# First mixer of a two-layer diffusion backbone: softmax division and gated rows on other engines, modulation sums at other rates

## The chip, the cores and the metric

The kernel runs on one core of a Trainium2 chip. The core has a matrix engine (TensorE, PE in the profile; its weight loads are listed apart as PEld), three engines for elementwise work (VectorE = DVE, ScalarE = ACT, GpSimd = POOL) and the queue engine SyncE (SP), which issues nearly all of this kernel's DMA transfers. Each engine runs its instructions in the order in which they stand in its own queue, and waits on semaphores for the others. TensorE writes to PSUM banks; VectorE and ScalarE read PSUM and SBUF, GpSimd only works on SBUF here. The metric is the device time of one execution, in microseconds; smaller is better.

## The reference, cut to what matters

One inference step of a backbone with two layers and width 2048, for 128 context tokens and 128 latent tokens side by side. The kernel carries both groups as the two halves of 256 columns (T = 128 each, NT = 256). Layer 0 is the one the change touches:

```python
mod = silu(cond) @ w_ada[l] + b_ada[l]           # cond: one row for each group
sh1, sc1, gt1, sh2, sc2, gt2 = split(mod, 6)      # each 2048 wide
h = rmsnorm(x, g_norm_mix[l]) * (1 + sc1) + sh1
m = mixer_ab(h)                                   # 8 MLA heads + 8 GQA heads, one output projection
x = x + gt1 * m                                   # "gated rows"
h = rmsnorm(x, g_norm_ffn[l]) * (1 + sc2) + sh2
x = x + gt2 * conv_ffn(h)
```
```python
s = einsum(q, k) * scale
p = softmax(s)           # exp(s - max) / sum     the division is by row
o = einsum(p, v)
```

The latent group also attends to 128 cached keys, so a head has scores of 128 columns for the first group and 256 for the second. Layer 1 has differential attention, and both layers end with a gated convolutional FFN. The output is x after a final RMSNorm, and the new context tensors.

## The kernel before

**Layout.** Features lie on the partitions: x is 16 chunks of [128, 256], one column for each token. Every weight matrix is streamed from HBM once in tiles of 1 MB (`Weights`, L263). For accuracy at the fast matmul format, each weight tile is split in two: a high half `wh` cast by ScalarE (L258) and the remainder `wl` = raw - `wh` by VectorE (L259); the activations are split in the same way. A product is then three matmuls for each 128x128 block: wh with the high activation, wh with the low, wl with the high (`gemm`). There are four `wh` and four `wl` buffers, each for 8 blocks.

**Order of work.** The kernel is written as a program, and a planner, which simulates the engines' time, orders each engine's queue. It may take instructions out of program order where their inputs are ready and a buffer is free; instructions handed to `keep_order` keep their relative order. Work beside the main stream is cut in steps that are called at fixed places: `pump(rate)` is called after each output chunk and adds `rate` to a due account, and whole steps are run from it.

**Modulation.** The vector `mod` has 12 x 2048 entries over both layers. One part ("rows") is computed by TensorE, with the condition as the weight and the matrix streaming (tile `araw`, result bank `ada`). Another part ("feature sums") is computed by VectorE: a tile of `w_ada` laid out with output features on partitions is multiplied with the condition row, and summed along the columns, one instruction for each group (L535, 128x1024, with a short instruction that reads the accumulator). `Deep` (L504) runs such sums within the mixers. For layer 0 it holds four units of 512 features (the shift of the FFN). The condition row is kept only for half the 2048 inputs at a time (`condb`), so each unit is summed in two halves: 32 sums with the first half of the row, a reload of the row with a SiLU on ScalarE, 32 sums with the second. Two sums (c = 0 and 1, the two groups) share one tile of 512 KB. With the six steps for the row and four finishing steps this makes 74 steps. `deep.rate` says how many steps one `pump` calls, from the table `SIDE` (L89). `deep.tiles` lists the buffers that the tiles take in turn: one (`block`) in the projection, two (`block`, `kvb`) in the heads, two (`block`, `more`) in the output projection.

**The first mixer.** `mixer_ab` projects the normalised x in four quarters of K; `Deep` starts in the last quarter (in3). Then come the heads, in four passes for two MLA heads and two GQA heads each: query products (`WQ`, from `ql`), key products and values (`WK`, from `kv_in`), scores, softmax, and the product with the values. `pump` is called seven times in a pass. `head_ab` (L907) is one head after its scores, written as a generator that is resumed by each `pump`: maxima on VectorE, exponentials with their sums on ScalarE, the reciprocal of the sums (L914) and the two multiplications of `p` by it (L915 and L916) on VectorE, then transposes of `p` on TensorE (in `transposed`, L891), a copy by ScalarE, and the product with v. In this stage two accumulator banks are in use.

**The output projection.** `out_ab` (L1336) multiplies the heads' output by `w_out_ab` for 16 chunks of 128 features. The first three chunks are interleaved (`first_three`), so that the heads that finish last are read last. Then one chunk follows the other, each with a full 1 MB tile. For each chunk, `residual` adds the gated product to x with one VectorE instruction for each group, out of PSUM (L856), and `stat_add` has its square made by ScalarE (L207) and added to an accumulator by GpSimd (L211). `rows(c)` writes the operand of the following FFN product from x (L712 on ScalarE, L715 on VectorE). `pump` is called once for each of the first 12 chunks. At chunk 12 `deep.flush()` runs whatever steps are left, and the last four chunks are prepared in smaller pieces.

Of the kernel before, what the change touches and what calls it, by code (L numbers as in the profile page):

```python
# [18 lines left out]
P = 128  # L19
D = 2048  # L20
KD = D // P
T = 128
# [63 lines left out]
RLIMIT = {"ab": 16, "ffn0": 17, "c": 22, "ffn1": 22}  # L86
FLIMIT = {"ab": 0, "ffn0": 12, "c": 12, "ffn1": 16}

SIDE = {"in3": 0.4, "heads": 1.6, "out0": 1.8, "c": 2.2, "outc": 2.0}  # L89
UW = NT + 2  # L90
INV = {2048: 0, 768: 1, 512: 2, 128: 3, 256: 4}

# [2 lines left out]
def step_kernel(ctx: ExitStack, tc: tile.TileContext, A: dict):  # L95
# [4 lines left out]
    def keep_order(i):  # L100
        if not any(i is j for j in kept):
            kept[:] = [i]
            tc.keep_in_program_order(i)
# [37 lines left out]
    def T_(pl, shape, tag, dt=F32, bufs=None):  # L141
        kw = {} if bufs is None else {"bufs": bufs}
        return pl.tile(shape, dt, tag=tag, name=nm(tag), **kw)
# [55 lines left out]
    def stat_add(st, src, n, eng=pool):  # L199

        st["n"] += 1
        if st["n"] == 1:
            st["acc"] = T_(keep, [P, NT], "sqacc")
            act.activation(st["acc"], src, AF.Square)
            return
        sq = T_(tmp, [P, NT], "sq", bufs=2)
        act.activation(sq, src, AF.Square)  # L207
        if st["n"] == n:
            st["last"] = sq
        else:  # L210
            eng.tensor_tensor(out=st["acc"], in0=st["acc"], in1=sq, op=ALU.add)  # L211
# [51 lines left out]
    class Weights:  # L263
# [11 lines left out]
        def load(self, parts=1, pin=lambda i: i):  # L275
            n = self.per
            if self.cycle:
                n = min(n, self.cycle - self.at * n % (-(-self.cycle // n) * n))
            n *= self.nblk if self.per < TB else 1
            raw = T_(wpool, [P, 4, 512], "raw").rearrange("p g n -> p (g n)")  # L280
            w = n * P // parts
            for i in range(parts):
                s = slice(i * w, (i + 1) * w)
                pin(sp.dma_start(out=raw[:, s], in_=self.src[self.at, :, s]))
            self.at += 1
            return raw, n
# [217 lines left out]
    class Deep:  # L504

        def __init__(self):
            self.steps, self.due, self.rate = [], 0.0, 0.0

        def begin(self, home, units, tiles, part, junk):
            self.home, self.tiles, self.part, self.junk, self.rate = home, tiles, part, junk, 0.0  # L510
            for half in range(2):
                if half:
                    self.steps += [lambda: self.cond(1)] + [lambda: None] * 3 + [self.silu, lambda: None]
                for i, u in enumerate(units):
                    for t in range(4):
                        for c in range(2):
                            self.steps.append(partial(self.sums, half, i, u, t, c))
                    if half:
                        self.steps.append(partial(self.finish, i, u))
# [7 lines left out]

        def sums(self, half, i, u, t, c):
            if c == 0:
                self.tiles.append(self.tiles.pop(0))  # L530
                self.raw = T_(self.tiles[0][0], [P, 2, 512], self.tiles[0][1])
                keep_order(sp.dma_start(out=self.raw, in_=A["w_ada"][u[0], u[1], u[2], t][:, 2 * half:2 * half + 2]))
            l, j, q = u
            out = self.part[:, i, t, c:c + 1] if half else mod[:, l, j, 4 * q + t, c:c + 1]
            keep_order(dve.tensor_tensor_reduce(  # L535
                out=self.junk, in0=self.raw, in1=self.row[:, c].rearrange("p (g n) -> p g n", g=2),
                scale=1.0, scalar=0.0, op0=ALU.mult, op1=ALU.add, accum_out=out))

        def finish(self, i, u):
            l, j, q = u  # L540
# [8 lines left out]
        def pump(self):  # L549
            self.due += self.rate  # L550
            while self.due >= 1.0:
                self.due -= 1.0
                if self.steps:
                    self.step()
# [298 lines left out]
    def residual(ps, l, which, c, st=None):  # L853
        for g in range(2):
            s = slice(g * T, (g + 1) * T)
            dve.scalar_tensor_tensor(out=x[:, c, s], in0=ps[:, s],  # L856
                                     scalar=mod[:, l, 3 * which + 2, c, g:g + 1],
                                     in1=x[:, c, s], op0=ALU.mult, op1=ALU.add)
        if st is not None:
            stat_add(st, x[:, c], KD)  # L860


    def rope(dst, src, heads, half, cn, sn):

        cb = C(cn)[:, None, :].to_broadcast([P, heads, T])
        sn_ = C(sn)
        t = T_(tmp, [P, 2, T], "rope", bufs=1)
        for a in range(0, P, 2 * half):
            lo, hi = slice(a, a + half), slice(a + half, a + 2 * half)
            for to, of in ((hi, lo), (lo, hi)):  # L870
                dve.tensor_tensor(out=t[to, :heads], in0=src[of],  # L871
                                  in1=sn_[of, None, :].to_broadcast([half, heads, T]), op=ALU.mult)
        dve.tensor_tensor(out=dst, in0=src, in1=cb, op=ALU.mult)
        dve.tensor_tensor(out=dst, in0=dst, in1=t[:, :heads], op=ALU.add)
# [32 lines left out]
    def head_ab(pl, s, rs, v, hx, c):  # L907

        mx = T_(small, [P, 2], "mx")
        sums = T_(small, [P, 2], "sums")  # L910
        p = T_(pl, [P, 3 * T], "p", bufs=3)
        softmax_parts(s, mx, sums, rs, None, p)
        rec = T_(small, [P, 2], "rec")
        dve.reciprocal(out=rec, in_=sums)  # L914
        dve.tensor_scalar(out=p[:, :T], in0=p[:, :T], scalar1=rec[:, 0:1], scalar2=None, op0=ALU.mult)  # L915
        dve.tensor_scalar(out=p[:, T:], in0=p[:, T:], scalar1=rec[:, 1:2], scalar2=None, op0=ALU.mult)  # L916
        yield
        yield
        pT = transposed(pl, p, bank)
        yield  # L920
        o = s
        pe.matmul(o[:, 0:T], v(0), pT[:, 0:T], start=True, stop=True)
        pe.matmul(o[:, T:NT], v(1), pT[:, T:2 * T], start=True, stop=False)
        pe.matmul(o[:, T:NT], v(2), pT[:, 2 * T:], start=False, stop=True)
        split(hx[:, c, :NT], hx[:, c, NT:2 * NT], o[:, :NT])


    def mixer_ab(hx, beside):
        l = 0
        with tc.tile_pool(name="ab", bufs=1) as ab:  # L930
# [307 lines left out]
            with tc.tile_pool(name="abh", bufs=1) as hp:  # L1238
# [63 lines left out]
                start(gqa_query(0))  # L1302
                deep.tiles.append((ab, "kvb"))
                deep.junk = o[:, 6:8]
                deep.rate = SIDE["heads"]
                for h in range(0, 8, 2):
                    for i in range(2):
                        ps = gemm(WQ.chunk(), qh, qlo)
                        qn[h + i] = T_(hp, [P, NT], "qn", bufs=4)
                        act.copy(qn[h + i], ps)  # L1310
                        pump(RATE["heads"])
                    ps = gemm(WQ.chunk(), qh, qlo)
                    if h == 6:
                        deep.junk = ql[:, 0:2]
                    ev = T_(tmp, [P, NT], "nt", bufs=4)
                    act.copy(ev, ps)
                    qr = T_(hp, [P, NT], "qr", bufs=2)
                    act.copy(qr[:, 0:T], ev[:, 0:T])
                    rope(qr[:, None, T:], ev[:, None, T:], 1, 32, "rcm", "rsm")
                    pump(RATE["heads"])  # L1320
                    kn = []
                    for i in range(2):
                        if h + i < 7:
                            start(gqa_query(h + i + 1))
                        start(gqa(h + i))
                        ps = gemm(WK.chunk(), kh, klo, 3 * T)
                        kn.append(T_(hp, [P, 3 * T], "kn", bufs=2))
                        act.copy(kn[i], ps)
                        pump(RATE["heads"])
                    mla_pair(h, qr, kn, values())  # L1330
# [5 lines left out]
    def out_ab(o, st, u, beside, rp):  # L1336
        l = 0
        rows = raw_rows(u, l, 1)
        ensure(l, 2)
        ada["pew"] = PEW["out0"]  # L1340
        W = Weights(A["w_out_ab"], KD, 1)
        oh, ol = (lambda k: o[:, k, :NT]), (lambda k: o[:, k, NT:2 * NT])
        deep.tiles = [(beside, "block"), (rp, "more")]
        deep.junk = u[:, 14:16, :512]
        deep.rate = SIDE["out0"]
        turn["acc"] = 0
        ready = first_three(W, oh, ol, PAIR_LATE, first=1, third=lambda: att_bank(0))
        for c in range(KD):
            fine[0] = c >= KD - QUIET[1]
            residual(ready.pop(0) if ready else gemm(W.chunk(), oh, ol, first=8), l, 0, c, st)  # L1350
            if c == KD - QUIET[1]:
                deep.flush()
            rows(c)
            pump(RATE["out0"] if c < KD - QUIET[1] else 0)

# [451 lines left out]
```

## Time and profile before

| | us |
|---|---|
| median of 3 runs | 2302.68 (2302.25 to 2302.72) |
| profiled execution | 2301.08 |
| its span, first to last instruction | 2299.3 |
| mean granted TensorE clock | 0.995 |
| last projection quarter (in3) | about 170 to 204 |
| heads | about 204 to 320 |
| output projection | about 320 to 433 |

The profile is of one execution. Busy times of TensorE are those of pipelined matmuls, so a TensorE that is shown as busy may still issue below its best rate; its waits and the granted clock are shown apart. A line number is that of the instruction in the kernel before. In rows with a count, the first number behind the bar is the group's busy time and the second the mean of one in ns.

### The profile page before, as it was taken

The numbers are of one execution on the slowest core, as the hardware profiler recorded it, in microseconds if no ns is written. First come the engines' busy times: TensorE is split into PE (matmuls) and PEld (weight loads), VectorE is DVE, ScalarE is ACT, GpSimd is POOL, SyncE is SP. The second block draws the span as 40 slices with busy tenths as digits, with TensorE's granted clock in tenths as the row PEclk, the third lists the DMA queues.
The fourth block names the chain that finished last, engine by engine and source line by source line (L and its number), as shares of the span: only waits on it lengthen the run. The fifth ranks groups of instructions, "written<-read, shape, count | busy, mean of one in ns | idle before, by whom it ended". The sixth has DMA issues, their size and how long they took to land.

```text
span 2299.3 us, 47506 instructions
## 1 busy us (share of the span) xinstructions
PE 2273.6 (99%) x19496; PEld 2181.4 (95%) x19496; DVE 1887.7 (82%) x3021; ACT 1197.0 (52%) x1991; POOL 176.1 (8%) x206
## 2 busy tenths in 40 slices
PE   9999999999999999999999999999999999999998
PEld 6788888999999999999999999999999999999998
DVE  4668978989989999999978988898899955666654
ACT  4445555665554355555575455457555434555543
POOL 0011101400000000001130000023000000000011
PEclk9999999999999999999999999999999999999999
DMA  9888889776777777777778888676677755555553
GB/s 395 361 347 310 325 311 346 271 289 247 269 265 285 286 278 261 258 272 258 283 288 303 319 323 313 255 282 222 251 254 264 259 202 189 197 194 191 199 188 127
DMA packets 100121, 617.14 MB, mean 268 GB/s; under 512 B 10752, under 2 KB 18880, under 8 KB 33344
## 3 DMA queue, kind: packets, MB, share of 16 engines
q1 hardware_dynamic: 99904, 614.11, 72.2%
q8 instruction: 153, 2.51, 0.4%
q14 instruction: 64, 0.52, 0.1%
HBM read 609.32 MB, written 4.75 MB: 267 GB/s over the span
## 4 chain that ended last, share of the span: by engine, by line
PE 79%; DVE 1%; POOL 1%; ACT 0%; issue 0%; DVEq 0%; ACTq 0%
PE acc L110 77%; PE att L110 1%; PE ada L110 1%; POOL dev L820 0%; PE att L113 0%; DVE x L1664 0%; POOL hxc L824 0%; DVE wl L259 0%; DVE dev L812 0%; PE ada L113 0%; DVE rope L871 0%; PE misc L110 0%; ACT dev L1425 0%; POOL rr L222 0%; DVE hx L259 0%
## 5 line engine op out<-in xcount | busy, mean ns | idle before, releaser
L110 PE MATMUL acc<-hx,wh 128*128 128x256 f32 (+1 forms) x7232 | 1250.5, 278 | 4.2 <-ACT wh L258 1.6
L258 ACT CAST wh<-raw 128x1024 fp32r<-128x1024 f32 (+1 forms) x866 | 798.7, 938 | 846.0 <-PE acc L110 709.3
L259 DVE TENSOR_TENSOR wl<-raw,wh 128x1024 fp32r<-128x1024 f32 (+1 forms) x866 | 927.9, 1089 | 243.0 <-ACT wh L258 235.9
L110 PEld LDWEIGHTS acc<-hx,wh 128*128 128x128 f32 x7232 | 1094.9, 188 | 24.6 <-issue 13.4
L110 PE MATMUL acc<-hx,wl 128*128 128x256 f32 (+1 forms) x3616 | 1003.5, 278 | 3.9 <-DVE wl L259 3.7
L110 PEld LDWEIGHTS acc<-hx,wl 128*128 128x128 f32 x3616 | 681.2, 188 | 6.9 <-DVE wl L259 5.1
L110 PE MATMUL acc<-g,wh 128*128 128x256 f32 x2816 | 478.8, 276 | 0.0
L110 PEld LDWEIGHTS acc<-g,wh 128*128 128x128 f32 x2816 | 423.7, 188 | 0.0
L110 PE MATMUL acc<-g,wl 128*128 128x256 f32 x1408 | 388.3, 276 | 0.0
L483 DVE CUSTOM_DVE_ANT_0 junk<-araw,condb 128x2048 f32<-128x2048 f32 x128 | 294.1, 2297 | 0.0
L110 PEld LDWEIGHTS acc<-g,wl 128*128 128x128 f32 x1408 | 264.2, 188 | 0.0
L211 POOL TENSOR_TENSOR sqacc<-sqacc,sq 128x256 f32<-128x256 f32 x62 | 73.4, 1184 | 1531.5 <-ACT sq L207 1526.1
L110 PE MATMUL acc<-hxc,wh 128*128 128x256 f32 (+1 forms) x1056 | 189.1, 281 | 0.0
L110 PEld LDWEIGHTS acc<-hxc,wh 128*128 128x128 f32 x1056 | 161.9, 188 | 1.8 <-issue 1.7
L110 PE MATMUL acc<-hxc,wl 128*128 128x256 f32 (+1 forms) x528 | 146.9, 278 | 0.0
L110 PEld LDWEIGHTS acc<-hxc,wl 128*128 128x128 f32 x528 | 99.5, 188 | 0.2
L110 PE MATMUL acc<-wh,hxc 128*128 128x256 f32 (+1 forms) x512 | 95.0, 283 | 0.8 <-DVE nt L831 0.8
L1557 ACT ACTIVATE cv<-acc,convw 128x256 f32<-128x256 f32 x169 | 94.2, 558 | 0.0
L1563 DVE SCALAR_TENSOR_TENSOR cv<-acc,convw,cv 128x254 f32<-128x254 f32 x169 | 80.8, 478 | 3.2
L110 PEld LDWEIGHTS acc<-wh,hxc 128*128 128x128 f32 x512 | 79.4, 188 | 3.7 <-issue 2.5
L856 DVE SCALAR_TENSOR_TENSOR x<-acc,mod,x 128x128 f32<-128x128 f32 x188 | 56.6, 342 | 31.3 <-PE acc L110 31.2
L535 DVE CUSTOM_DVE_ANT_0 hx<-block,condb 128x1024 fp32r<-128x1024 f32 x62 | 75.5, 1218 | 6.8 <-ACT condb L526 4.3
(288 smaller groups left out, 1814.8 us busy)
## 6 DMA issues: line engine op xcount, KB each, us to landing
raw<-w_up SPq DMA_DIRECT2D x176, 1024.0 KB, 4.8
araw<-w_ada SPq DMA_DIRECT2D x132, 1024.0 KB, 6.1
raw<-w_down SPq DMA_DIRECT2D x88, 1024.0 KB, 4.8
raw<-w_in_c SPq DMA_DIRECT2D x48, 1024.0 KB, 6.9
block<-w_ada SPq DMA_DIRECT2D x41, 512.0 KB, 6.8
raw<-w_in_ab SPq DMA_DIRECT2D x18, 1024.0 KB, 9.2
raw<-w_out_ab SPq DMA_DIRECT2D x16, 1024.0 KB, 8.1
raw<-w_out_c SPq DMA_DIRECT2D x16, 1024.0 KB, 7.3
```

Of the source, the lines that this page charges most:

```text
L110: return self.placed(nc.tensor.matmul(*a, **kw))
L211: eng.tensor_tensor(out=st["acc"], in0=st["acc"], in1=sq, op=ALU.add)
L258: pin(act.copy(out_hi, src))
L259: pin(dve.tensor_tensor(out=out_lo, in0=src, in1=out_hi.bitcast(F32), op=ALU.subtract))
L483: keep_order(dve.tensor_tensor_reduce(out=T_(feat["pool"], [P, D], "junk"), in1=feat["row"][:, c], in0=feat["raw"].rearrange("p g n -> p ( ...
L535: keep_order(dve.tensor_tensor_reduce(out=self.junk, in0=self.raw, in1=self.row[:, c].rearrange("p (g n) -> p g n", g=2), scale=1.0, scala ...
L856: dve.scalar_tensor_tensor(out=x[:, c, s], in0=ps[:, s], scalar=mod[:, l, 3 * which + 2, c, g:g + 1], in1=x[:, c, s], op0=ALU.mult, op1=AL ...
L1557: pin(act.activation(y, ps, AF.Identity, scale=cw[:, 1, m:m + 1], bias=cw[:, 3, m:m + 1]))
L1563: pin(dve.scalar_tensor_tensor(out=y3[:, :, :T - 1], in0=p3[:, :, 1:], scalar=cw[:, 2, m:m + 1], in1=y3[:, :, :T - 1], op0=ALU.mult, op1=A ...
```

## The change

Five edits, all in the first mixer:

1. In `head_ab`, the two multiplications by the reciprocal become ScalarE activations with a scale, and stand behind the first `yield` instead of ahead of it.
2. In `out_ab`, chunks 0 to 11 use the new `gated`: two ScalarE multiplications out of PSUM into a scratch tile, and one GpSimd addition to x. Chunks 12 to 15 keep `residual`.
3. The rates of the sums are 0.5, 1.9 and 1.85 for 0.4, 1.6 and 1.8.
4. In the last pass of the heads, after the query products, `deep.settle()` runs the sums that are begun or whose tile is loaded, and sets the rate to 0; the rate of the output projection is set only at its chunk 2.
5. `Deep` keeps a list of tiles to load. With `ahead` set, the load of the next tile is issued in the program behind the first sum of a tile, instead of ahead of the next tile's first sum.

```diff
--- before.py
+++ after.py
@@ -86,7 +86,7 @@
 RLIMIT = {"ab": 16, "ffn0": 17, "c": 22, "ffn1": 22}
 FLIMIT = {"ab": 0, "ffn0": 12, "c": 12, "ffn1": 16}
 
-SIDE = {"in3": 0.4, "heads": 1.6, "out0": 1.8, "c": 2.2, "outc": 2.0}
+SIDE = {"in3": 0.5, "heads": 1.9, "out0": 1.85, "c": 2.2, "outc": 2.0}
 UW = NT + 2
 INV = {2048: 0, 768: 1, 512: 2, 128: 3, 256: 4}
 
@@ -505,6 +505,7 @@
 
         def __init__(self):
             self.steps, self.due, self.rate = [], 0.0, 0.0
+            self.loads, self.got, self.mid, self.ahead = [], [], False, False
 
         def begin(self, home, units, tiles, part, junk):
             self.home, self.tiles, self.part, self.junk, self.rate = home, tiles, part, junk, 0.0
@@ -513,6 +514,7 @@
                     self.steps += [lambda: self.cond(1)] + [lambda: None] * 3 + [self.silu, lambda: None]
                 for i, u in enumerate(units):
                     for t in range(4):
+                        self.loads.append((half, u, t))
                         for c in range(2):
                             self.steps.append(partial(self.sums, half, i, u, t, c))
                     if half:
@@ -527,14 +529,29 @@
 
         def sums(self, half, i, u, t, c):
             if c == 0:
-                self.tiles.append(self.tiles.pop(0))
-                self.raw = T_(self.tiles[0][0], [P, 2, 512], self.tiles[0][1])
-                keep_order(sp.dma_start(out=self.raw, in_=A["w_ada"][u[0], u[1], u[2], t][:, 2 * half:2 * half + 2]))
+                if not self.got:
+                    self.load()
+                self.raw = self.got.pop(0)
+            self.mid = c == 0
             l, j, q = u
             out = self.part[:, i, t, c:c + 1] if half else mod[:, l, j, 4 * q + t, c:c + 1]
             keep_order(dve.tensor_tensor_reduce(
                 out=self.junk, in0=self.raw, in1=self.row[:, c].rearrange("p (g n) -> p g n", g=2),
                 scale=1.0, scalar=0.0, op0=ALU.mult, op1=ALU.add, accum_out=out))
+            if c == 0 and self.ahead and self.loads:
+                self.load()
+
+        def load(self):
+            half, u, t = self.loads.pop(0)
+            self.tiles.append(self.tiles.pop(0))
+            raw = T_(self.tiles[0][0], [P, 2, 512], self.tiles[0][1])
+            keep_order(sp.dma_start(out=raw, in_=A["w_ada"][u[0], u[1], u[2], t][:, 2 * half:2 * half + 2]))
+            self.got.append(raw)
+
+        def settle(self):
+            self.ahead, self.rate = False, 0.0
+            while self.got or self.mid:
+                self.step()
 
         def finish(self, i, u):
             l, j, q = u
@@ -860,6 +877,14 @@
             stat_add(st, x[:, c], KD)
 
 
+    def gated(ps, l, which, c, st):
+        t = T_(tmp, [P, NT], "nt", bufs=4)
+        for g in range(2):
+            s = slice(g * T, (g + 1) * T)
+            act.activation(t[:, s], ps[:, s], AF.Identity, scale=mod[:, l, 3 * which + 2, c, g:g + 1])
+        pool.tensor_tensor(out=x[:, c], in0=x[:, c], in1=t, op=ALU.add)
+        stat_add(st, x[:, c], KD)
+
     def rope(dst, src, heads, half, cn, sn):
 
         cb = C(cn)[:, None, :].to_broadcast([P, heads, T])
@@ -912,9 +937,9 @@
         softmax_parts(s, mx, sums, rs, None, p)
         rec = T_(small, [P, 2], "rec")
         dve.reciprocal(out=rec, in_=sums)
-        dve.tensor_scalar(out=p[:, :T], in0=p[:, :T], scalar1=rec[:, 0:1], scalar2=None, op0=ALU.mult)
-        dve.tensor_scalar(out=p[:, T:], in0=p[:, T:], scalar1=rec[:, 1:2], scalar2=None, op0=ALU.mult)
         yield
+        act.activation(p[:, :T], p[:, :T], AF.Identity, scale=rec[:, 0:1])
+        act.activation(p[:, T:], p[:, T:], AF.Identity, scale=rec[:, 1:2])
         yield
         pT = transposed(pl, p, bank)
         yield
@@ -1302,7 +1327,7 @@
                 start(gqa_query(0))
                 deep.tiles.append((ab, "kvb"))
                 deep.junk = o[:, 6:8]
-                deep.rate = SIDE["heads"]
+                deep.rate, deep.ahead = SIDE["heads"], True
                 for h in range(0, 8, 2):
                     for i in range(2):
                         ps = gemm(WQ.chunk(), qh, qlo)
@@ -1318,6 +1343,8 @@
                     act.copy(qr[:, 0:T], ev[:, 0:T])
                     rope(qr[:, None, T:], ev[:, None, T:], 1, 32, "rcm", "rsm")
                     pump(RATE["heads"])
+                    if h == 6:
+                        deep.settle()
                     kn = []
                     for i in range(2):
                         if h + i < 7:
@@ -1342,14 +1369,17 @@
         oh, ol = (lambda k: o[:, k, :NT]), (lambda k: o[:, k, NT:2 * NT])
         deep.tiles = [(beside, "block"), (rp, "more")]
         deep.junk = u[:, 14:16, :512]
-        deep.rate = SIDE["out0"]
         turn["acc"] = 0
         ready = first_three(W, oh, ol, PAIR_LATE, first=1, third=lambda: att_bank(0))
         for c in range(KD):
             fine[0] = c >= KD - QUIET[1]
-            residual(ready.pop(0) if ready else gemm(W.chunk(), oh, ol, first=8), l, 0, c, st)
+            add = residual if fine[0] else gated
+            add(ready.pop(0) if ready else gemm(W.chunk(), oh, ol, first=8), l, 0, c, st)
+            if c == 2:
+                deep.rate, deep.ahead = SIDE["out0"], True
             if c == KD - QUIET[1]:
                 deep.flush()
+                deep.ahead = False
             rows(c)
             pump(RATE["out0"] if c < KD - QUIET[1] else 0)
 
```

## The prediction

> **What bounds the kernel now.** I read the page first: one TensorE stream, and a chain of waits that is TensorE nearly throughout.
>
> ```profile
> span 2299.3 us, 47506 instructions
> PE 2273.6 (99%) x19496; PEld 2181.4 (95%) x19496; DVE 1887.7 (82%) x3021; ACT 1197.0 (52%) x1991; POOL 176.1 (8%) x206
> PE 79%; DVE 1%; POOL 1%; ACT 0%; issue 0%; DVEq 0%; ACTq 0%
> ```
>
> The change neither adds nor removes a matmul, so it can only win what TensorE loses to waits and to a low clock in the stages it touches: last quarter of the projection, heads, output projection (about 180 to 433 us). So I read next TensorE's waits from 200 to 440 us (total, times, longest), then stretches (for each engine busy us and count, then granted clock, DMA share, GB/s).
>
> ```profile
> PE acc L110 <- DVE wl L259: 3.0, 2, 2.7
> PE att L110 <- ACT sq L207: 1.1, 1, 1.1
> PE acc L110 <- ACT vm L1279: 0.3, 1, 0.3
> PE acc L110 <- ACT wh L258: 0.2, 1, 0.2
> ```
> ```profile
> 200.00:320.00 120.00, 120.00 (x898) 98.00 (x897) 100.25 (x267) 68.63 (x161) 14.11 (x16) 1.00 0.86 325
> ...
> 356.00:433.00 77.00, 77.00 (x665) 71.93 (x664) 71.75 (x131) 39.17 (x73) 15.04 (x12) 1.00 0.86 322
> ```
> ```profile
> 345.20:348.60 3.40, 1.67 (x12) 0.60 (x4) 3.40 (x11) 2.60 (x6) 1.19 (x1) 1.00 0.99 352
> 348.60:355.40 6.80, 5.71 (x27) 5.71 (x27) 5.50 (x10) 2.50 (x8) 1.24 (x1) 0.50 0.99 377
> ...
> 432.00:435.40 3.40, 2.27 (x20) 2.18 (x20) 3.40 (x10) 1.69 (x6) 0.00 (x0) 1.00 0.37 154
> ```
>
> The heads (200 to 320) and the body of the output projection (356 to 433) keep TensorE full while VectorE is busy 84% and 93%: VectorE is crowded there but sets no end. All that is to be had lies at the seam, where the output projection's fourth tile is prepared. In all 3.0 + 1.1 + 0.3 + 0.2 = 4.6 us of waits, and from 348.6 to 355.4 half the clock: 5.71 us of work that takes 2.9 us at full clock, 2.9 us lost. The seam on TensorE, ScalarE and VectorE:
>
> ```profile
> 345.86 0.50 PE L110 MATMUL acc<-hx,wh 128*128 128x256 f32 x2
> 346.52 0.50 PE L110 MATMUL acc<-hx,wh 128*128 128x256 f32 x2 [0.16 <-ACT wh L258]
> 349.69 0.58 PE L110 MATMUL acc<-hx,wl 128*128 128x256 f32 x1 [2.66 <-DVE wl L259]
> ```
> ```profile
> 343.53 2.94 ACT L258 CAST wh<-raw 128x1024 fp32r<-128x1024 f32 x3 [3.52 <-PE acc L110]
> ```
> ```profile
> 344.56 1.23 DVE L535 CUSTOM_DVE_ANT_0 ql<-kvb,condb 128x1024 fp32r<-128x1024 f32 x1 [0.40 <-DMA kvb<-w_ada]
> ...
> 345.71 1.12 DVE L856 SCALAR_TENSOR_TENSOR x<-acc,mod,x 128x128 f32<-128x128 f32 x4
> 346.75 1.21 DVE L535 CUSTOM_DVE_ANT_0 ql<-kvb,condb 128x1024 fp32r<-128x1024 f32 x1
> ...
> 347.89 0.60 DVE L856 SCALAR_TENSOR_TENSOR x<-att,mod,x 128x128 f32<-128x128 f32 x2
> 348.41 2.35 DVE L259 TENSOR_TENSOR wl<-raw,wh 128x1024 fp32r<-128x1024 f32 x2
> ```
>
> ScalarE makes three high halves one after another, so the first stands after a third of 2.94 us, at 344.5. Its low half (L259) starts only at 348.41: ahead of it on VectorE are two feature sums (L535) and the gated rows of chunks 0 to 2 (L856, six instructions, 1.72 us). TensorE stands 2.66 us for it.
>
> **The change part by part.**
>
> *None at the heads' end.* In steps of the deep queue (74: 64 sums, 6 for the condition row, 4 finishes): before, 16 pumps x 0.4 and 28 x 1.6 issue 51 by the heads' end, and out0 goes on at once. After, 16 x 0.5 + 24 x 1.9 = 53.6 by the third pump of the last pair; settling brings 55, that is 48 sums. Then nothing until chunk 2, and 0.6 + 10 x 1.85 = 19.1 takes the last 19 by chunk 11. If VectorE keeps up, the two sums at the seam are gone. Their work goes into the heads, beside a full TensorE.
>
> *Gated rows.* Chunks 0 to 11: 24 of L856 leave VectorE; each takes 0.28 us (1.12 / 4). Come: 24 ScalarE multiplies of 128 columns out of PSUM and 12 GpSimd adds. At the seam this takes off VectorE the 1.72 us that stood ahead of the low half, and puts six multiplies on ScalarE, where the casts start at 343.53.
>
> ```profile
> L712 ACT ACTIVATE u<-x,scl 128x128 fp32r<-128x128 f32 x28 | 10.7, 393 | 2.3 <-DVE x L856 1.6 <-DVE mod L535 0.7
> ```
> ```profile
> L887 ACT ACTIVATE p<-att,nmx,rsb 128x128 f32<-128x128 f32 x8 | 3.7, 461 | 4.3 <-DVE nmx L885 4.3
> L1252 ACT ACTIVATE qb<-qb,cst 128x256 f32<-128x256 f32 x6 | 3.1, 510 | 0.2
> ```
>
> Between 0.39 (same function, from SBUF) and 0.46 us (Exp from PSUM) I take 0.39, the same function: six are 2.4 us. Placed wholly ahead of the casts they make the first low half 2.4 us late (bound: all of the gain at the seam), wholly behind them nothing. ScalarE idled 3.52 us before those casts, and chunk 0 is done first, so I let one multiply stand in front: 0.3 to 0.4 us, kept as a loss of 0.3. In the body, 9 chunks x 2 x 0.39 = 7.1 us on ScalarE (39 of 77 us busy) cost nothing.
>
> *The GpSimd adds* have the form of the square sums on the same engine. What they do to VectorE:
>
> ```profile
> L211 POOL TENSOR_TENSOR sqacc<-sqacc,sq 128x256 f32<-128x256 f32 x62 | 73.4, 1184 | 1531.5 <-ACT sq L207 1526.1
> ```
> ```profile
> 378.72 1.07 POOL L211 TENSOR_TENSOR sqacc<-sqacc,sq 128x256 f32<-128x256 f32 x1 [4.49 <-ACT sq L207]
> ```
> ```profile
> 379.12 1.75 DVE L535 CUSTOM_DVE_ANT_0 u<-more,condb 128x1024 fp32r<-128x1024 f32 x1
> ```
>
> A sum that takes 1.22 us takes 1.75 beside such an add. Twelve more adds can thus cost VectorE up to 12 x 0.53 = 6.4 us of the 24 x 0.28 = 6.7 that it is spared: **no relief in the body**. Nor does it need any; there are also 16 sums there in place of 20. The square of a row, and the raw row made of it, now wait on ScalarE for the add, with casts behind them: a microsecond or two. TensorE holds up to four cast half tiles of 8 blocks x 3 matmuls x 0.116 us (77 / 665) = 2.8 us each, so this hides; with that cover gone it would be the add's 1.2 us a chunk.
>
> *Division.* 16 heads x two scalings (L915, L916: 0.6 us a head) leave VectorE and come to ScalarE: 16 x (0.39 + 0.51) = 14.4 us there.
>
> ```profile
> 329.82 0.28 DVE L915 TENSOR_SCALAR p<-p,rec 128x128 f32<-128x128 f32 x1
> 330.02 0.34 DVE L916 TENSOR_SCALAR p<-p,rec 128x256 f32<-128x256 f32 x1
> ```
>
> ScalarE has 51 of 120 us free in the heads, so I price it at nothing; bounds 0 and 14.4 us (fully exposed). The scaling waits for VectorE's reciprocal; behind it on ScalarE stand the copies that free two accumulators, for which TensorE would wait.
>
> *Rates.* Tile loads (32, and two of the condition row) stay the same in number; on SP's queue those of the sums leave the stretch in which the output projection's tiles are loaded, which gains nothing, as no wait in the list above is for a DMA. Can the sums keep the pace? Two records each, so x60 is 30 sums:
>
> ```profile
> 206.00:301.00 95.00, 36.76 (x60) 1.00 0.88 331
> 301.00:318.00 17.00, 0.00 (x0) 1.00 0.91 371
> 318.00:349.00 31.00, 14.62 (x24) 0.99 0.74 267
> ```
>
> Before, 44 of 64 have run by 349 (the twenty in out0 follow), two of them ahead of 206. The new kernel must run 48 by about 341: 46 in 341 - 206 - 17 = 118 us, 2.6 us each. Before, the pace was 95 / 30 = 3.2 and after the condition row 31 / 12 = 2.6. Two tiles allow (6.9 + 2 x 1.22) / 4 = 2.3 (landing below). The division frees 16 x 0.6 us besides. So it can just be met; this is the thinnest step.
>
> *Loaded one sum ahead.* With two tiles in turn the load already leaves when its tile comes free: the sum ends at 326.25 + 1.22 = 327.47 and the load follows at 327.50. Price 0. VectorE's, SyncE's rows, and the time to landing of the sums' loads in the heads:
>
> ```profile
> 326.25 1.22 DVE L535 CUSTOM_DVE_ANT_0 hx<-kvb,condb 128x1024 fp32r<-128x1024 f32 x1
> ...
> 335.13 1.23 DVE L535 CUSTOM_DVE_ANT_0 ql<-kvb,condb 128x1024 fp32r<-128x1024 f32 x1 [3.42 <-DMA kvb<-w_ada]
> ...
> 336.28 0.69 DVE L259 TENSOR_TENSOR wl<-raw,wh 128x512 fp32r<-128x512 f32 x1
> ```
> ```profile
> 327.50 0.33 SPq L532 DMA_DIRECT2D kvb<-w_ada  x1
> ```
> ```profile
> DMA to landing us min/median/max: 4.3/6.9/10.0
> ```
>
> That same load held VectorE 3.42 us and the low half behind it: the other 0.4 us wait on wl, which the quiet end also removes.
>
> **The sum.** Waits for wl 3.0 and half clock 2.9 go, 0.3 comes for the casts: -5.6 us. The waits on vm and on the last square (chunks 12 to 15 keep the old rows) stay. Profiled execution 2301.08 - 5.6 = 2295.5; the median of the runs lies 1.6 us above the profiled one, so **2297.1**. The half clock is in the sum because it starts at 348.6, inside the wait, and no other wait here is followed by one: 3.40 us with 1.67 busy led to it, 3.40 with 2.27 busy (432 to 435.4) did not.
>
> The Trainium skill, "TensorE: Matmul & The Clock Gate", Part 1, says that the clock halves after an idle window of about 3.4 us; by that a wait of 2.66 us would not cause it, and the sum would be -2.7. The trace disagrees: the longest idle in that stretch is 2.66 us, and the clock was 0.50 behind it.
>
> **The rivals.**
> - *The seam's wait changes hands* (24%). The sums miss the pace (at 3.2 us each only 37 of 46 are done by 341), or ScalarE runs the six multiplies ahead of the casts: TensorE then waits up to 2.4 us for wh in place of wl, and the clock halves again. For: casts and multiplies become ready at the same moment. Against: without L856 the low half is 1.72 us earlier even with both sums in place, and a wait of about 0.9 us keeps the clock. Gain 0 to 3: about 2301.2.
> - *Slower: sums wait for their tiles on VectorE in the heads* (17%). At 1.9 a pump (120 us / 28 pumps = 4.3 us) a sum is due every 2.3 us and a tile every 9.0; a tile takes 6.9 + 2.4 = 9.3. A sum placed ahead of its landing holds VectorE as at 335.13, there with low halves behind it. For: the 3.42 us hold. Against: most such holds cost TensorE nothing. One seam-like stall (2.66 + 2.9 = 5.6) cancels the gain; from two on the kernel is slower: 2302.7 - 5.6 + 11.2 = 2308.3.
> - *The clock stays low there whatever happens to the wait* (4%): -3.0 + 0.3, 2300.0.
>
> **How the numbers follow.** The forecast gets 55%. Its own range goes from every wait and the clock gone (4.6 + 2.9 = 7.5: 2295.2), with 1 us for row sums that fall elsewhere, 2294.2, to 2299. The whole range, 2294.2 to 2304.0, takes in the first and third rival and the near end of the second. A change of 0.2% is 4.6 us, about what a measurement of this kernel can tell from none. The forecast lies only 1 us beyond it, so a seventh of its chance (8%) falls within; with 25 of the 28% of the two gainless rivals (the other 3 are faster) and 3 of the 17% of the slower one (a single stall): same 0.36, faster 0.55 - 0.08 + 0.03 = 0.50, slower 0.14.
>
> **What would show it.** Right: no feature sum between the heads' last matmul and chunk 2's row, the wait for wl under 1 us, clock 1.00 from 346 to 356, TensorE still 120.00 of 120.00 in the heads. Wrong: sums still beside the fourth tile (pace); a wait for wh with multiplies ahead of the casts (order on ScalarE); new waits for evictions or low halves between 210 and 340; a half clock in the heads. VectorE's operations of 1.75 us in the output projection should about double in number.

## The result and the profile after

The changed kernel takes 2295.53 us (median of 7, 2294.64 to 2296.02) against 2302.68: ratio 0.9969, 95% interval 0.9960 to 0.9979, or 7.15 us. Its profiled execution took 2295.23 us, 5.85 under that of before. First its page, then TensorE's waits from 200 to 440 us, then stretches as in the prediction.

```profile
span 2293.4 us, 47509 instructions
PE 2272.2 (99%) x19496; PEld 2180.4 (95%) x19496; DVE 1880.7 (82%) x2963; ACT 1215.1 (53%) x2049; POOL 190.9 (8%) x219
```
```profile
PE acc L110 <- ACT kn L1355: 0.8, 1, 0.8
PE att L110 <- ACT sq L207: 0.5, 1, 0.5
```
```profile
200.00:320.00 120.00, 119.23 (x885) 97.05 (x883) 99.29 (x250) 78.46 (x192) 13.07 (x16) 1.00 0.88 324
...
341.00:346.00 5.00, 5.00 (x46) 4.46 (x48) 3.21 (x5) 2.12 (x4) 0.47 (x1) 1.00 0.63 241
346.00:356.00 10.00, 10.00 (x87) 8.01 (x80) 9.71 (x16) 7.41 (x19) 7.21 (x5) 1.00 0.86 342
356.00:433.00 77.00, 76.55 (x662) 72.36 (x661) 68.90 (x118) 45.71 (x100) 25.65 (x23) 1.00 0.84 320
```

Waits fell from 4.6 to 1.3 us, and the half clock (2.9 us) is gone: 6.2 us, against 5.85 between the profiled executions. The heads pay 0.8 us for a copy (`kn`) that ScalarE makes late; where it comes from is told below. VectorE is hardly emptier there (99.29 of 120 us, 100.25 before): sums, 35 for 31 in this stretch, filled most of what the division left. The seam, on VectorE and ScalarE:

```profile
340.71 1.22 DVE L538 CUSTOM_DVE_ANT_0 ql<-kvb,condb 128x1024 fp32r<-128x1024 f32 x1
...
341.97 1.23 DVE L538 CUSTOM_DVE_ANT_0 ql<-kvb,condb 128x1024 fp32r<-128x1024 f32 x1
...
344.96 1.23 DVE L259 TENSOR_TENSOR wl<-raw,wh 128x1024 fp32r<-128x1024 f32 x1 [1.75 <-ACT wh L258]
346.42 3.12 DVE L259 TENSOR_TENSOR wl<-raw,wh 128x1024 fp32r<-128x1024 f32 x2 [0.23 <-PE ada L110]
349.47 1.75 DVE L538 CUSTOM_DVE_ANT_0 ql<-block,condb 128x1024 fp32r<-128x1024 f32 x1
```
```profile
343.88 1.05 ACT L258 CAST wh<-raw 128x1024 fp32r<-128x1024 f32 x1 [3.60 <-PE acc L110]
344.83 0.62 ACT L884 ACTIVATE nt<-acc,mod 128x128 f32<-128x128 f32 x2
345.34 1.04 ACT L258 CAST wh<-raw 128x1024 fp32r<-128x1024 f32 x1
346.28 0.64 ACT L884 ACTIVATE nt<-acc,mod 128x128 f32<-128x128 f32 x2
346.79 1.06 ACT L258 CAST wh<-raw 128x1024 fp32r<-128x1024 f32 x1
```

VectorE now waits 1.75 us for the high half and starts the low half at once. But the sums are not finished at the heads' end, as the pause meant them to be: two run right up to the cast, and two more at 349.47, after the seam. Whether the pause does the work is therefore open from this profile alone, and so is which of the five edits does.

### The profile page after: what moved, and what is told of

The parts are those of the page before. It is cut to its first block, busy times and chain, and to the rows that moved or that the text cites. A ratio compares the mean times of both kernels' runs of the same rounds, so it can differ in the third digit from the quotient of the medians.

```text
span 2293.4 us, 47509 instructions
## 1 busy us (share of the span) xinstructions
PE 2272.2 (99%) x19496; PEld 2180.4 (95%) x19496; DVE 1880.7 (82%) x2963; ACT 1215.1 (53%) x2049; POOL 190.9 (8%) x219
## 4 chain that ended last, share of the span: by engine, by line
PE 96%; DVE 1%; DMA 1%; ACT 1%; POOL 1%; issue 0%; SPq 0%; DVEq 0%; ACTq 0%
PE acc L110 89%; PE ada L110 3%; PE att L110 2%; DMA raw<-w_in_ab 1%; PE misc L110 0%; DVE wl L259 0%; DMA araw<-w_ada 0%; PE att L113 0%; POOL dev L837 0%; PE ada L113 0%; PE misc L113 0%; ACT wh L258 0%; DVE x L1694 0%; POOL hxc L841 0%; DVE qb L1184 0%
## 5 line engine op out<-in xcount | busy, mean ns | idle before, releaser
L538 DVE CUSTOM_DVE_ANT_0 hx<-block,condb 128x1024 fp32r<-128x1024 f32 x66 | 80.4, 1218 | 4.7 <-DMA block<-w_ada 4.4
L1593 DVE SCALAR_TENSOR_TENSOR cv<-acc,convw,cv 128x254 f32<-128x254 f32 x169 | 80.8, 478 | 3.2
L1590 DVE SCALAR_TENSOR_TENSOR cv<-acc,convw,cv 128x254 f32<-128x254 f32 x169 | 80.2, 474 | 0.0
```

The lines of the kernel that those rows point to most:

```text
L538: keep_order(dve.tensor_tensor_reduce(out=self.junk, in0=self.raw, in1=self.row[:, c].rearrange("p (g n) -> p g n", g=2), scale=1.0, scala ...
L1590: pin(dve.scalar_tensor_tensor(out=y3[:, :, 1:], in0=p3[:, :, :T - 1], scalar=cw[:, 0, m:m + 1], in1=y3[:, :, 1:], op0=ALU.mult, op1=ALU.add))
L1593: pin(dve.scalar_tensor_tensor(out=y3[:, :, :T - 1], in0=p3[:, :, 1:], scalar=cw[:, 2, m:m + 1], in1=y3[:, :, :T - 1], op0=ALU.mult, op1=A ...
```

## The experiments

The four theories in the expectations: **A**, the prediction's own (the seam is cleared by the gated rows and the pause; the division is worth nothing); **B**, VectorE's relief counts in proportion; **C**, the multiplies delay the casts; **D**, formed after the first runs: the division carries the seam, and the sums must be done before the last chunks. All times are medians; "before" is the kernel before in the same session.

### The parts alone

Gated rows alone: the kernel before with the function `gated` of the change, used for chunks 0 to 11 (its definition is left out here).

```diff
-            residual(ready.pop(0) if ready else gemm(...), l, 0, c, st)
+            add = residual if fine[0] else gated
+            add(ready.pop(0) if ready else gemm(...), l, 0, c, st)
```

> The kernel before with the gated rows of chunks 0 to 11 on ScalarE and GpSimd, and nothing else of the change. Theory A (the gain is the seam's wait with the half clock behind it, and whatever takes 1.7 us off VectorE ahead of the fourth tile's low half is enough): the wait for wl falls from 2.66 us to about 1 us, no half clock from 346 to 356, time 4.0 to 5.0 us under the kernel before (about 2298). Theory B (the relief of VectorE over the whole stage counts, in proportion): the GpSimd adds give back 0.53 us for each 0.56 us spared, so within 1 us of before. Theory C (the multiplies delay the casts): a wait for wh of 1 to 2.4 us takes the place of the wait for wl, half clock stays, within 1.5 us of before.

Measured 2300.31 against 2301.81; ratio 0.9994 (0.9985 to 1.0003): no gain that can be told. Its waits, and the seam on VectorE:

```profile
PE acc L110 <- DVE wl L259: 2.9, 1, 2.9
```
```profile
344.68 1.23 DVE L535 CUSTOM_DVE_ANT_0 ql<-kvb,condb 128x1024 fp32r<-128x1024 f32 x1 [0.40 <-DMA kvb<-w_ada]
...
345.95 1.63 DVE L535 CUSTOM_DVE_ANT_0 ql<-kvb,condb 128x1024 fp32r<-128x1024 f32 x1
...
347.51 5.08 DVE L259 TENSOR_TENSOR wl<-raw,wh 128x1024 fp32r<-128x1024 f32 x3
```

The gated rows are off VectorE, yet the wait is 2.9 us. The low half starts 0.9 us earlier than before (347.51 for 348.41), but the second sum takes 1.63 us for 1.21 before, and each low half 1.69 (5.08 / 3) for 1.22, while GpSimd adds the three rows. So theory A's condition "whatever takes 1.7 us off VectorE" is refuted.

Division alone:

```diff
-        dve.tensor_scalar(out=p[:, :T], in0=p[:, :T], scalar1=rec[:, 0:1], scalar2=None, op0=ALU.mult)
-        dve.tensor_scalar(out=p[:, T:], in0=p[:, T:], scalar1=rec[:, 1:2], scalar2=None, op0=ALU.mult)
         yield
+        act.activation(p[:, :T], p[:, :T], AF.Identity, scale=rec[:, 0:1])
+        act.activation(p[:, T:], p[:, T:], AF.Identity, scale=rec[:, 1:2])
```

> The kernel before with the division on ScalarE alone. Theory A: nothing at the seam changes directly, the sums are at most 2 or 3 earlier; within 1.5 us of before with the half clock still there, unless the sums' order at the seam shifts. Theory B (VectorE's relief in proportion: about 10 of the 21 us of VectorE time that the change moves): 3 us under before.

Measured 2302.86 against 2301.81; 1.0004 (0.9996 to 1.0013). The time says nothing happened; the profile says otherwise. Its waits, then the seam and the end of the output projection as stretches:

```profile
PE acc L110 <- DVE u L736: 1.8, 1, 1.8
PE att L110 <- ACT sq L207: 1.4, 1, 1.4
PE acc L110 <- ACT u L735: 1.1, 1, 1.1
PE att L110 <- POOL rr L222: 0.7, 1, 0.7
```
```profile
345.00:360.00 15.00, 15.00 (x128) 11.53 (x126) 14.24 (x25) 8.72 (x18) 4.11 (x3) 1.00 0.86 330
432.00:437.00 5.00, 2.12 (x14) 1.52 (x12) 5.00 (x15) 3.67 (x12) 2.71 (x4) 1.00 0.49 195
437.00:443.80 6.80, 6.04 (x28) 6.04 (x29) 5.88 (x14) 6.79 (x21) 6.70 (x12) 0.50 0.01 2
```

The seam is clear: no wait for wl, clock 1.00 from 345 to 360. The gain is lost again in a **new stall 90 us later**: TensorE waits for the shift columns (L735, L736), which need the last feature sums, and the clock halves from 437 to 444. On VectorE:

```profile
430.62 1.21 DVE L535 CUSTOM_DVE_ANT_0 u<-block,condb 128x1024 fp32r<-128x1024 f32 x1
...
431.88 1.23 DVE L535 CUSTOM_DVE_ANT_0 u<-block,condb 128x1024 fp32r<-128x1024 f32 x1
...
437.42 0.29 DVE L736 TENSOR_TENSOR u<-mod,u 128x8 fp32r<-128x8 f32 x1
```

In the kernel before, the last sum and L736 come at nearly the same times, but TensorE has no wait for them, because it comes to that place about 5 us later:

```profile
431.95 1.21 DVE L535 CUSTOM_DVE_ANT_0 u<-block,condb 128x1024 fp32r<-128x1024 f32 x1
437.91 0.16 DVE L736 TENSOR_TENSOR u<-mod,u 128x8 fp32r<-128x8 f32 x1
```

So the division alone did not bring the end of the sums forward; it brought TensorE forward to meet it.

The sums' part alone: the changed kernel with both moves undone (`residual` for every chunk, the division on VectorE).

> The changed kernel with division and gated rows back on VectorE: only the sums' rates, the pause at the heads' end and the early loads. Theory A: if the sums keep the pace the seam is free of them and the low half waits only behind 1.7 us of gated rows: wait about 1 us, no half clock, 4 to 5 us under before. If they miss the pace, the seam still has sums and the time is within 1.5 us of before. Theory B: more sums in the heads with no relief there, slower by 1 to 3 us.

Measured 2305.79 against 2301.81; 1.0015 (1.0006 to 1.0024), 4 us slower. TensorE waited 7.3 us for ScalarE's cast of the last heads' output, the wait that is shown below for the changed kernel without the division (the profiled execution took 2308.82 us, the longest of the 11). Both moves together, sums as before:

> The kernel before with division and gated rows moved, the sums as before. Theory A: like the gated rows alone, 4 to 6 us under before; the division adds nothing. Theory B: the sum of the two parts alone, each in proportion.

Measured 2302.99 against 2301.81; 1.0005 (0.9996 to 1.0014). Seam clear, and the same waits for the shift columns (1.6 us on L736, 0.6 on L735). The clock is at half from 432 to 442; it falls before these waits, behind one of 1.3 us for the last square. No part alone, nor both moves together, can be told to be faster.

### The change with one part taken out

Without the division (only the two lines back on VectorE):

> The changed kernel with only the division back on VectorE. Theory D (the division is what lets the sums keep the pace, so that none stands ahead of the low half at the seam; the gated rows do little): the sums slip, the seam gets its stall and a half clock back, as in the sums' part alone: at least 4 us slower than the changed kernel, 2300 to 2306. Theory A (gated rows plus the pause are enough, division is worth nothing): within 1.5 us of the changed kernel.

Measured 2303.42 against 2301.54; 1.0008 (0.9999 to 1.0017): the whole gain is lost. It is not lost to the stall that was expected at the seam, but to another wait (6.6 us), again with half the clock behind it. VectorE, ScalarE and TensorE at the heads' end:

```profile
345.69 1.23 DVE L538 CUSTOM_DVE_ANT_0 hx<-block,condb 128x1024 fp32r<-128x1024 f32 x1 [3.81 <-DMA block<-w_ada]
...
346.96 1.23 DVE L538 CUSTOM_DVE_ANT_0 hx<-block,condb 128x1024 fp32r<-128x1024 f32 x1
```
```profile
348.23 0.37 ACT L258 CAST hx<-att 128x256 fp32r<-128x256 f32 x1 [11.61 <-DVE mod L538]
```
```profile
348.65 0.79 PE L110 MATMUL acc<-hx,wh 128*128 128x256 f32 x2 [6.64 <-ACT hx L258]
```

The cast waits for a feature sum because the sums issued in the heads leave their unused products in chunks 6 and 7 of the very tile that the last two heads write (`deep.junk = o[:, 6:8]`). A sum that runs late holds those heads back. With the division on ScalarE the pace is enough. The last sum with the first half of the condition row starts at 293.58 in the changed kernel and at 298.62 without the division, at the same rates of the program:

```profile
293.58 1.22 DVE L538 CUSTOM_DVE_ANT_0 hx<-block,condb 128x1024 fp32r<-128x1024 f32 x1
```
```profile
298.62 1.22 DVE L538 CUSTOM_DVE_ANT_0 hx<-block,condb 128x1024 fp32r<-128x1024 f32 x1
```

The reload of the row and its SiLU stand behind that sum, and the lead grows there: the first sum with the second half starts at 308.15 for 317.52, and by 344 us 46 sums have started for 42.

The 0.8 us that TensorE loses in the heads come from the same place. ScalarE, in the changed kernel:

```profile
304.91 1.28 ACT L528 ACT_TABLE_LOAD   x1
306.21 1.92 ACT L528 ACTIVATE condb<-condb 128x2048 f32<-128x2048 f32 x1
...
308.40 1.28 ACT L912 ACT_TABLE_LOAD   x1
...
310.69 0.47 ACT L1355 COPY kn<-acc 128x384 f32<-128x384 f32 x1
```

The SiLU, with a table load of 1.28 us on each side of it, now stands ahead of a copy that TensorE needs; without the division the first of these loads starts at 314.28, behind the copies. The division alone has no such wait.

Without the gated rows (`residual` in all chunks):

> The changed kernel with the gated rows back on VectorE in all chunks. Theory D (VectorE gets back from the gated rows only what the GpSimd adds cost it, and ScalarE is freed): within 1.5 us of the changed kernel, no half clock between 330 and 440. Theory A: a wait of 1.7 us for the low half comes back at the seam, 2 to 5 us slower.

Measured 2294.31 against 2301.54; 0.9971 (0.9959 to 0.9982): the gain is all there. Between 200 and 445 us TensorE has one wait left, the 0.8 us for a copy. Without the early loads (`ahead` left False):

> The changed kernel without the loads one sum ahead. Theory A and D (a load leaves when its tile comes free, whatever its place in the program): within 1 us of the changed kernel. Rival (the early load is what feeds the higher rate): VectorE waits for tiles in the heads, 2 us slower or more.

Measured 2294.94 against 2301.54; 0.9974 (0.9964 to 0.9984): the same.

Without the pause and the early loads. Here the heads' rate is 1.93, and the output projection's rate is set at its start:

```diff
-                    if h == 6:
-                        deep.settle()
...
-            if c == 2:
-                deep.rate = SIDE["out0"]
```

> The changed kernel without the pause at the heads' end and without the early loads (the heads' rate 1.93 in place of 1.9, so that no tile is half summed where the buffers change). If the pause is what keeps sums away from the seam: sums between 343 and 348 ahead of the low half, wait and half clock at the seam, 4 us or more slower than the changed kernel. If division and rates are enough: within 1.5 us of it.

Measured 2294.58 against 2301.37; 0.9975 (0.9966 to 0.9984): the same. Its profiled execution was the longest of the 11, 2299.30 us, but the waits between 200 and 445 us are those of the others (0.8 us for the copy). On VectorE the next sum stands behind the low halves although nothing holds it there by rule:

```profile
345.60 1.23 DVE L259 TENSOR_TENSOR wl<-raw,wh 128x1024 fp32r<-128x1024 f32 x1 [3.23 <-ACT wh L258]
347.07 1.44 DVE L259 TENSOR_TENSOR wl<-raw,wh 128x1024 fp32r<-128x1024 f32 x1 [0.24 <-ACT wh L258]
348.43 1.75 DVE L538 CUSTOM_DVE_ANT_0 ql<-block,condb 128x1024 fp32r<-128x1024 f32 x1
```

So the pause as such is not needed, and the changed kernel's pause had not ended the sums either. The least that was run, division, rates and pause only:

> Only division, rates and pause: the changed kernel without gated rows and without early loads. Theory D: within 1 us of the changed kernel, perhaps 1 us faster, with no half clock. Theory A: a wait at the seam, 2 us slower or more.

Measured 2294.55 against 2301.37; 0.9971 (0.9960 to 0.9982). It is not to be told from the changed kernel (0.9969), with much less code. Two of the five edits carry the gain: division and rates. Each is needed (without the division 2303.42; both moves with the rates as before 2302.99). Every kernel that was run with these two has either the pause or the gated rows besides; the two by themselves were not run.

### What eats the gain at the far end

First, the kernel before with the division moved and a higher rate in the output projection alone (the lines of the division are left out here):

```diff
-SIDE = {"in3": 0.4, "heads": 1.6, "out0": 1.8, "c": 2.2, "outc": 2.0}
+SIDE = {"in3": 0.4, "heads": 1.6, "out0": 2.0, "c": 2.2, "outc": 2.0}
```

> The kernel before with the division on ScalarE and the output projection's rate of sums 2.0 in place of 1.8, so that 12 pumps run all 23 steps that are left and none is flushed at chunk 12. Theory D (the division alone clears the seam, and what it lost again was the last sums finishing beside the last chunks, so that the shift columns came late): the waits on the shift columns (L735, L736) and the half clock at 437 to 444 go, 5 to 7 us under the kernel before. Rival (VectorE at the end of the output projection is simply full): the waits stay, within 2 us of the kernel before.

Measured 2302.64 against 2301.54; 1.0004 (0.9995 to 1.0013). Theory D's expectation missed: the stall stayed, 1.8 us on L736. But the condition was not met, since the sums hardly ended earlier: the last one starts at 431.1 (431.9 with the rate of 1.8). At this place the higher rate in the program did not set the pace. So the amount of work was cut in place of its rate, with the division moved as well:

```diff
-                    for t in range(4):
+                    for t in range(2 if half and u == (0, 3, 3) else 4):
```

> The kernel before with the division on ScalarE, and the last four feature sums left out (the second half of unit (0,3,3) is summed over two of its four tiles, the rest is taken as zero, so the shift of the first FFN is not the reference's there). Theory D (the division alone clears the seam; what ate its gain is that the last sums still run beside the last chunks, so that the shift columns come late and the clock halves): the waits on L735 and L736 and the half clock at 437 go, 6 to 8 us under the kernel before. Rival (the end of the output projection stalls for another cause, such as the division's changed order): waits and half clock stay, within 2 us of before.

Measured 2294.84 against 2301.37; 0.9973 (0.9962 to 0.9983), 6.5 us faster. Four sums are 4.9 us of VectorE work, and two tile loads of 512 KB go with them; TensorE's work is the same. (The shift of the FFN is incomplete in this kernel.) The last sum, and the same stretch as above:

```profile
421.71 1.21 DVE L535 CUSTOM_DVE_ANT_0 u<-block,condb 128x1024 fp32r<-128x1024 f32 x1
```
```profile
432.00:437.00 5.00, 5.00 (x45) 3.59 (x43) 4.32 (x11) 4.34 (x12) 3.57 (x6) 1.00 0.19 75
437.00:443.80 6.80, 6.80 (x59) 6.64 (x56) 6.66 (x16) 6.80 (x20) 6.57 (x9) 1.00 0.98 377
```

No wait is left between 200 and 445. Theory D holds in this part: with a clear seam, a last sum at 431.1 or later cost what the division won. The changed rates do the same without leaving anything out: there the last sum starts at 423.2, and at 424.9 without the early loads, also with no wait for the shift columns.

### The clock by itself

The kernel before, with 24 matmuls more that nothing uses:

```diff
+            if c == 3:
+                filler = bank()
+                for k in range(24):
+                    keep_order(pe.matmul(filler[:, :NT], o[:, k % 4, :P], o[:, k % 4, :NT], start=True, stop=True))
```

> The kernel before with 24 extra matmuls (about 2.7 us at full clock, into a bank that nothing reads) ahead of the fourth chunk's product. If the half clock comes from TensorE's idle time in the wait, and the extra work fills that wait: clock 1.00 from 346 to 356, the wait gone or under 0.5 us, 2 to 3 us under the kernel before although it does more. If the half clock has another cause: it stays, and the time is that of before or up to 2.7 us more.

Measured 2297.60 against 2301.37; 0.9985 (0.9976 to 0.9994): **more work, 3.8 us less time**. TensorE at the seam, and the stretch that had half the clock:

```profile
344.19 3.13 PE L110 MATMUL misc<-hx 128*128 128x256 f32 x24
347.15 0.63 PE L110 MATMUL acc<-hx,wh 128*128 128x256 f32 x4
348.89 0.38 PE L110 MATMUL acc<-hx,wl 128*128 128x256 f32 x1 [1.10 <-DVE wl L259]
```
```profile
348.60:355.40 6.80, 6.51 (x58) 5.72 (x62) 6.80 (x12) 2.96 (x5) 1.25 (x1) 1.00 1.02 388
```

The extra matmuls fill most of the wait, 1.10 us of it are left, and the clock stays at 1.00. On VectorE two sums still stand ahead of the low half (343.74 and 345.93, the low half at 347.59), so the half clock follows TensorE's idleness there. Not all of the 3.8 us is the clock, however: the wait on the last square (1.1 us before) has gone too, and the planner's order moved with the edit, so that the last sum starts at 423.05 for 431.95.

## Why the prediction was right or wrong

**Time: right, and by the right mechanism on TensorE.** Forecast 2297.1, measured 2295.53, within the forecast's own range. What the sum took away, the waits for wl and the half clock, is what went; the filler shows that the clock belongs in it. The rest of the sum came close by luck: the 0.3 us for the casts did not come (the cast at 343.88 stands ahead of the multiplies), the waits on vm, wh and the last square fell by 1.1 us, and 0.8 us came in the heads. **By which edits: wrong, and there the number was lucky.** The sum credited the gated rows and the pause, and each of them can be taken out of the change; it gave nothing to the division, without which there is no gain.

**Division, priced at nothing: wrong step.** It is the edit without which there is no gain (2303.42). The step looked at where the 14.4 us go on ScalarE, where it was right (with the division alone ScalarE is busy 77.61 of the 120 us of the heads and TensorE 120.00), and not at what VectorE does with the time. The "Rates" step had it in half a sentence ("frees 16 x 0.6 us besides"); there it was the deciding term.

**Gated rows: wrong step.** They were to bring 1.72 us at the seam; alone they leave a wait of 2.9 us, and taking them out of the change costs nothing. The same part said that GpSimd's adds take back from VectorE what they spare, and limited that to the body. It holds at the seam too. The multiply itself took 0.36 us (0.39 taken), and the adds are slow. From 360 to 433 us VectorE is busy 65.91 us with the gated rows and 66.75 without them. Its operations of 1.6 to 1.8 us between 345 and 433 us went from 6 to 9, where the prediction expected about double.

```profile
L884 ACT ACTIVATE nt<-acc,mod 128x128 f32<-128x128 f32 x24 | 7.4, 359 | 0.0
```
```profile
L885 POOL TENSOR_TENSOR x<-x,nt 128x256 f32<-128x256 f32 x13 | 17.0, 1311 | 64.5 <-ACT nt L884 61.6 <-ACT u L752 2.9
```

**None at the heads' end: wrong step.** The sums did not end at 341, as the pace step feared: 46 of the 48 have started by 342, two of them between the heads and chunk 2, and the other two follow the low halves. The pause can be taken out. The sums' higher rates matter, but at the other end of the output projection, 90 us on, of which the prediction said only that the wait on the last square stays; it did not name the shift columns at all.

**Loaded one sum ahead, priced at 0: right** (2294.94 without).

**The rivals.** The first rival's result, no gain and a half clock again, is what the gated rows alone show, but with the wait still on wl; in the whole change it did not occur. The slower rival saw that a missed pace costs more than it can gain, and the sums' part alone was slower (4 us), with VectorE held 3.9 us for a tile. But TensorE did not wait for low halves in the heads: it waited for the last heads' output, through the tile in which the sums leave their products. That the clock stays low is refuted.

**What stays open.** Why the division puts the low halves ahead of the sums at the seam. By itself it does not do so by pace: in the kernel before and with the division alone, 42 sums have started by 344 us, and the next two start at 344.56 and 346.75, ahead of the low half, in the one, and at 348.07 and 351.42, behind it, in the other. In the kernels with it, the last sums ahead of the cast start at 339 to 343 and the next at 347 or later; in those without, two to five start between 343 and 353. The planner's order and the times of the tiles' loads both move with the division, and no run separates them.

## What to carry to other kernels

When an engine that sets no end is relieved, ask what it will do with the time and what comes due downstream: here 10 us off VectorE were worth nothing alone, because TensorE then met a stall 90 us on, and 7 us together with work scheduled to be done before that place. An edit's part must therefore be tested by taking it out of the whole as well as by adding it alone. Where a short wait is followed by half a clock, filling it with useless matmuls is a cheap test of what the clock costs.

## What the runs showed of the hardware that was not expected

A wait of 2.66 to 2.9 us in one piece was followed by half of TensorE's clock for 6.8 us (before) and some 3.4 us (gated rows alone: 350.6 to 354.1, a stretch granted 0.51); a wait of 1.1 us was not, neither in the kernel before nor with the filler. Between these, the length of the one wait does not decide. Behind a wait of 1.36 us for the last square the clock halved (division with the rate of 2.0, the row from 430.4 below); behind a wait of 1.37 us at the same place it did not (division alone, the last row). The first row is that of the gated rows alone.

```profile
350.60:354.10 3.50, 3.50 (x20) 3.50 (x19) 3.50 (x7) 1.31 (x2) 2.51 (x2) 0.51 0.98 353
```
```profile
430.40:433.80 3.40, 3.40 (x18) 3.40 (x17) 3.40 (x9) 2.42 (x6) 1.67 (x1) 0.51 0.82 272
```
```profile
430.30:433.70 3.40, 2.73 (x23) 2.52 (x22) 3.40 (x8) 1.71 (x4) 1.67 (x1) 1.00 0.58 173
```

GpSimd's additions of two SBUF tiles slow VectorE's two-input operations: in the kernel before, 13 of the 14 additions between 345 and 433 us lengthened one such operation beside them by about 0.53 us (1.22 to 1.75). With twelve more, moving rows off VectorE bought next to nothing there.
